# RWKV recurrence: the triangular inverse by substitution in 16x16 blocks and one Newton step

## The chip, the cores and the metric

One core of a Trainium2 chip runs the whole program. The metric is device time in microseconds, the median of the runs shown; lower is better. TensorE (PE), VectorE (DVE), ScalarE (ACT), GpSimd (POOL) and the DMA queues (issued mostly by SP) each work through their own list of instructions in order and meet through semaphores.

## What is computed

The reference is a stack of transformer blocks in float32. Its first part has an attention layer, an RWKV-7 layer and two MLPs; a second part follows with further mixers and feed-forward layers. The change touches the RWKV-7 recurrence alone, which runs over 256 context tokens and 512 tokens, in both directions, for 16 heads of 64:

```python
def wkv_scan(r, w, k, v, a, b, s0, reverse):
    def step(s, inp):
        r_t, w_t, k_t, v_t, a_t, b_t = inp
        sa = jnp.einsum('bhvk,bhk->bhv', s, a_t)
        s = s * w_t[:, :, None, :] + sa[..., None] * b_t[:, :, None, :] + v_t[..., None] * k_t[:, :, None, :]
        return s, jnp.einsum('bhvk,bhk->bhv', s, r_t)
```

## The kernel before

The recurrence is computed in chunks of 64 tokens: 12 chunks ("slots") per direction and head. Inside a chunk the dependence of each step on the ones before it is a strictly triangular 64x64 matrix A, and the chunk needs the inverse of (I - A). `rwkv_wkv` (L1789) makes 8 passes, one for each pair of heads. A pass has 2 directions x 2 heads x 12 slots = 48 such matrices; direction d lies in partitions 64d to 64d + 63.

For a pass, `wkv_scores` (L1950) makes the matrices A and masks them into `GA` (VectorE, L1973) and the output factors into `E` (L1975). `wkv_inverse` (L2043) inverts the two 32x32 diagonal blocks of each matrix. It copies them into `Z` (ScalarE, L2048), transposes them on VectorE so that each of the 128 partitions holds one row index of the 24 matrices side by side (L2051, L2052), and then substitutes forward: 30 steps of a multiplication into `pr` (L2061) and an addition into `T` (L2062). Two transposes bring the result back as `TC` and as its turned form `TS` (L2066, L2067), and four copies on ScalarE put it on the diagonal of `TTt` (L2073). `wkv_cross` (L2077) then makes the off-diagonal 32x32 block of the 64x64 inverse with two groups of products of 32x32 matmuls, on two of the array's strips at a time (L2086 and L2087, L2098 and L2099), and evicts them on ScalarE and VectorE. After it come `wkv_transfer` (L2105: `pswu`, `psft`, the evictions `FC` and `FT`), `wkv_scan` (L2142: 11 chained steps `pstep` with the eviction `S` on ScalarE, and the outputs `psy` to `Y`) and, in the next pass, `wkv_readout` (L2205, partly on GpSimd).

The inverse of pass p + 1 is made during pass p. The order is written by hand: a string of letters, `WKV_ORDER` (L1451), or `WKV_LAST` (L1454) for the last pass, says which generator takes its next step, and `in_order` (L1855) spreads the steps of the inverse evenly between the letters:

```python
            while done < 34 and done * n <= 34 * j:
                next(inverse, None)
                done += 1
            if c in steps:
                with self.tc.issue_after(last):
                    next(steps[c], None)
```

Here y is the cross product, b the transposes of `BK` (`psbk`, L2037), m the products `psmv` (L2026), w the transfer, s the scan, z the readout of the pass before, g the scores, a and v two more sets of transposes. The recording layer may still move an instruction ahead of others on its engine. `TC` and `TS` share their buffers with tiles of the readout (tags `zz` and `ro`, one buffer each), and PSUM results rotate over six banks (`psum`, L1910). In the pass before the last, g is the last part of `ada`, a vector-matrix product whose weights are loaded then.

## Time and profile before

| | |
|---|---|
| median of 3 runs | 3828.26 us (3827.4 to 3834.72) |
| the profiled execution | 3828.17 us, span 3826.0 us |
| PE busy | 3610.4 us, 94% of the span |
| DVE busy | 2059.8 us, 54% |
| ACT busy | 1583.4 us, 41% |
| POOL busy | 728.8 us, 19% |

The span runs from the first to the last instruction of the profiled execution; the device time has a little around it. A busy share is an average over stages that differ in what holds them up. The recurrence takes about 500 us of the span, from about 1390 us on. A matmul of float32 operands leaves two MATMUL records in the trace, and its end is modelled, so records of neighbouring matmuls overlap: how fast a group runs is read from the distance of starts.

### The profile page before, as it was taken

What the parts mean: (1) busy time and instruction counts of PE and PEld (TensorE: products, weight loads), DVE (VectorE), ACT (ScalarE), POOL (GpSimd) and SP (SyncE); (2) the same over time, 40 slices, a digit from 0 to 9 for tenths busy, and PEclk for the clock granted to TensorE, in tenths of its full rate; (3) what the DMA queues carried; (4) which work ended last, traced back from release to release, by engine and by line L of the source; (5) the groups of instructions that cost most, each with busy time, mean ns of one, the idle gap of its engine ahead of it and who ended that gap; (6) DMA issues with size and microseconds to landing.
All of it is one profiled execution on the core that took longest, in us unless ns stands there. A gap on an engine that the chain in (4) does not pass through costs nothing.

```text
span 3826.0 us, 62818 instructions
## 1 busy us (share of the span) xinstructions
PE 3610.4 (94%) x25700; PEld 2920.4 (76%) x25700; DVE 2059.8 (54%) x3993; ACT 1583.4 (41%) x2988; POOL 728.8 (19%) x602
## 2 busy tenths in 40 slices
PE   7999999999898978888899999998999899989998
PEld 5777877888775657777688889888888788778886
DVE  5556433333557778778354345567434734474346
ACT  5555332122334656765442234354222444442233
POOL 2000033434212010001134430003111200031112
PEclk9999999999999988888899999999999999999999
DMA  5232233122232772232433332113333211133332
GB/s 180 64 94 96 73 101 99 60 67 63 73 106 93 272 267 75 94 94 88 156 103 94 94 99 84 44 57 100 92 96 100 88 59 53 53 92 90 99 96 69
DMA packets 308272, 370.76 MB, mean 97 GB/s; under 512 B 31768, under 2 KB 228368, under 8 KB 305936
## 3 DMA queue, kind: packets, MB, share of 16 engines
q1 hardware_dynamic: 298752, 340.28, 28.2%
q0 software_dynamic: 8976, 26.40, 2.2%
q8 instruction: 202, 3.31, 0.4%
q14 instruction: 86, 0.70, 0.1%
q10 hardware_dynamic: 256, 0.07, 0.0%
HBM read 324.72 MB, written 41.98 MB: 96 GB/s over the span
## 4 chain that ended last, share of the span: by engine, by line
PE 53%; DVE 9%; ACT 3%; issue 2%; DMA 1%; POOL 0%; SPq 0%; DVEq 0%; ACTq 0%; POOLq 0%
PE psu L144 5%; PE psu L143 5%; PE psu L142 5%; PE psy L144 5%; PE psy L143 4%; PE psy L142 4%; PE psj L144 4%; PE psj L143 4%; PE psj L142 4%; DVE T L2062 2%; PE S L973 2%; DVE pr L2061 2%; DVE Tlo L298 1%; ACT Z L2048 1%; PE psk L142 1%
## 5 line engine op out<-in xcount | busy, mean ns | idle before, releaser
L136 ACT CAST whi<-wraw 128x1024 fp32r<-128x1024 f32 (+1 forms) x402 | 417.0, 1039 | 922.0 <-PE psy L144 527.6
L137 DVE TENSOR_TENSOR wlo<-wraw,whi 128x1024 fp32r<-128x1024 f32 (+1 forms) x402 | 506.4, 1262 | 535.2 <-ACT whi L136 534.8
L142 PE MATMUL psu<-Thi,whi 128*128 128x512 f32 (+1 forms) x1408 | 498.5, 354 | 8.7 <-ACT r L334 6.0
L144 PE MATMUL psu<-Thi,wlo 128*128 128x512 f32 (+1 forms) x1408 | 500.0, 355 | 0.3 <-DVE wlo L137 0.3
L143 PE MATMUL psu<-Tlo,whi 128*128 128x512 f32 (+1 forms) x1408 | 497.9, 354 | 0.0
L142 PE MATMUL psj<-whi,Thi 128*128 128x256 f32 (+1 forms) x1568 | 482.1, 309 | 8.3 <-ACT whi L136 6.1
L144 PE MATMUL psj<-whi,Tlo 128*128 128x256 f32 (+1 forms) x1568 | 475.1, 304 | 2.9 <-DVE Tlo L298 2.6
L143 PE MATMUL psj<-wlo,Thi 128*128 128x256 f32 (+1 forms) x1568 | 475.9, 304 | 1.7 <-DVE wlo L137 1.6
L142 PE MATMUL psy<-whi,uh 128*128 128x512 f32 x1152 | 452.5, 393 | 2.8 <-ACT whi L136 2.7
L144 PE MATMUL psy<-whi,ul 128*128 128x512 f32 x1152 | 454.6, 395 | 0.0
L143 PE MATMUL psy<-wlo,uh 128*128 128x512 f32 x1152 | 452.1, 392 | 0.5 <-DVE wlo L137 0.5
L335 POOL TENSOR_TENSOR q<-r 128x512 f32<-128x512 f32 (+1 forms) x176 | 235.3, 1337 | 876.7 <-ACT r L334 876.6
L142 PEld LDWEIGHTS psj<-whi,Thi 128*128 128x128 f32 x1568 | 300.1, 192 | 23.1 <-ACT whi L136 7.2
L144 PEld LDWEIGHTS psj<-whi,Tlo 128*128 128x128 f32 x1568 | 299.2, 191 | 17.0 <-DVE Tlo L298 4.3
L143 PEld LDWEIGHTS psj<-wlo,Thi 128*128 128x128 f32 x1568 | 299.9, 191 | 15.2 <-DVE wlo L137 3.6
L142 PEld LDWEIGHTS psu<-Thi,whi 128*128 128x128 f32 x1408 | 266.9, 190 | 52.0 <-ACT r L334 8.1
L143 PEld LDWEIGHTS psu<-Tlo,whi 128*128 128x128 f32 x1408 | 267.1, 190 | 40.7
L144 PEld LDWEIGHTS psu<-Thi,wlo 128*128 128x128 f32 x1408 | 266.7, 189 | 38.6 <-DVE wlo L137 0.7
L337 DVE TENSOR_TENSOR ul<-q,uh 128x512 fp32r<-128x512 f32 (+1 forms) x176 | 104.6, 595 | 312.2 <-ACT uh L336 311.9
L144 PEld LDWEIGHTS psy<-whi,ul 128*128 128x128 f32 x1152 | 216.6, 188 | 52.9 <-DVE ul L337 6.5
L142 PEld LDWEIGHTS psy<-whi,uh 128*128 128x128 f32 x1152 | 216.8, 188 | 51.8 <-ACT whi L136 3.9
L143 PEld LDWEIGHTS psy<-wlo,uh 128*128 128x128 f32 x1152 | 216.6, 188 | 47.8 <-DVE wlo L137 0.8
(549 smaller groups left out, 6209.4 us busy)
## 6 DMA issues: line engine op xcount, KB each, us to landing
wraw<-in_mlp_w_dram SPq DMA_DIRECT2D x128, 512.0 KB
wraw<-in_ffn_w_dram SPq DMA_DIRECT2D x128, 512.0 KB
wraw<-in_ada_w_dram SPq DMA_DIRECT2D x64, 512.0 KB
wraw<-in_ev_w_in_dram SPq DMA_DIRECT2D x28, 512.0 KB
scr_bk<-BK SPq DMA_DIRECT2D x16, 768.0 KB
wraw<-in_od_w_in_dram SPq DMA_DIRECT2D x24, 512.0 KB
BK<-scr_bk SPq DMA_DIRECT2D x14, 768.0 KB
wraw<-in_rwkv_w_rkv_dram SPq DMA_DIRECT2D x16, 512.0 KB
```

The source lines that it names most:

```text
L136: nc.scalar.copy(hi, raw)
L137: nc.vector.tensor_tensor(lo, raw, hi.bitcast(F32), SUB)
L142: mm(ps, lhsT=ah, rhs=bh, start=start, stop=False)
L143: mm(ps, lhsT=ah, rhs=bl, start=False, stop=False)
L144: mm(ps, lhsT=al, rhs=bh, start=False, stop=stop)
L298: nc.vector.tensor_tensor(lo[k][:, s], t[:, :w], hi[k][:, s].bitcast(F32), SUB)
L335: nc.gpsimd.tensor_tensor(q[:, :w], r[:, :w], r[:, :w], MUL)
L337: nc.vector.tensor_tensor(ul[:, o:o + w], q[:, :w], uh[:, o:o + w].bitcast(F32), SUB)
L973: nc.tensor.matmul(S[:, :W], lhsT=q, rhs=k, start=True, stop=True)
L2048: nc.scalar.copy(Z[q, :, 0:24], GA[d][q, :, :, 32 * bl:32 * bl + 32].rearrange("p h s t -> p t (h s)"))
L2061: nc.vector.tensor_tensor(pv, T[:, j + 1:, j:j + 1].to_broadcast([P, n, j]), T[:, j:j + 1, 0:j].to_broadcast([P, n, j]), MUL)
L2062: nc.vector.tensor_tensor(T[:, j + 1:, 0:j], T[:, j + 1:, 0:j], pv, ADD)
```

## The change

VectorE now substitutes only in the two 16x16 diagonal blocks of each 32x32 block, both at once: 14 steps, over a view `B` of `T` that has the two blocks as one dimension. So `TC` and `TS` hold a block diagonal matrix X. A new generator, `wkv_merge`, makes the inverse of the 32x32 blocks by one Newton step, X (2I - (I - A) X), which is exact here because only one off-diagonal block is missing. For each head it accumulates 2I, -X and A X in one bank (`psn1`), with wide matmuls against the constant `two` and one 32x32 matmul per slot and strip, copies that to SBUF, multiplies it by X (`psn2`) and evicts the result straight into `TTt`; for the two strips that the cross product reads, it also makes the turned form (`psn3`) and writes it back into `TS` and `TC`. The four strips of the array take a matmul each in turn. The merge is made at the start of the pass itself, as four steps with the letter x ahead of the y steps. The four copies of L2073 are gone.

```diff
@@ -1448,10 +1448,10 @@
 
 
 
-WKV_ORDER = ("z b y b y b m y b m y b z b w w l z m w z m w s w z s w z s w w s w z s z z z s g v s g a s g s g v s g a "
+WKV_ORDER = ("x z x b x b x b y m y b y m y b z b w w l z m w z m w s w z s w z s w w s w z s z z z s g v s g a s g s g v s g a "
              "s g g v s g g a s g k r g g")
 
-WKV_LAST = "y m y m y y z w w z m w m z s w w s z w s z s w w w s s z s z z s z s r s q s q s q s q s"
+WKV_LAST = "x z x m x m x y y y y w w z m w m z s w w s z w s z s w w w s s z s z z s z s r s q s q s q s q s"
 LAST_PARTS = ((0, 4), (4, 8))
 WKV_FIRST = "f f f f f f f f b b b b b b"
 WKV_START = "l A A A v v v k c c . . . g g a g g c a g g c a g g c g g c g g c c c c"
@@ -1791,6 +1791,11 @@
         with ExitStack() as s:
             cp = self.pool(s, "wc", 1)
             self.Z = cp.tile([P, 32, 32], F32, name="Z")
+            self.two = cp.tile([P, 2, 32], F32, name="two")
+            for i in range(4):
+                q = slice(32 * i, 32 * i + 32)
+                for j, f in enumerate((2.0, -1.0)):
+                    nc.vector.tensor_scalar(self.two[q, j, :], self.ident[q, q], f, None, MUL)
 
             self.IR = cp.tile([P, 8, 3, 64], F32, name="IR")
 
@@ -1838,7 +1843,7 @@
                     pb = self.pb.pop()
                     bank = lambda name: pb.tile([P, 512], F32, name=name, tag="b")
                     ada = self.ada(1, (2,), bank, lambda: self.lt([P, 4, 2, 64], "DC").rearrange("p c i t -> p (c i t)"), self.wkv_raws)
-                steps = dict(m=self.wkv_fill_m(u[p]), y=self.wkv_cross(u[p]), w=self.wkv_transfer(u[p]), s=self.wkv_scan(u[p]), z=self.wkv_readout(u[p - 1]) if p else iter(()),
+                steps = dict(x=self.wkv_merge(u[p]), m=self.wkv_fill_m(u[p]), y=self.wkv_cross(u[p]), w=self.wkv_transfer(u[p]), s=self.wkv_scan(u[p]), z=self.wkv_readout(u[p - 1]) if p else iter(()),
                              l=self.wkv_next(u), k=self.wkv_next_v(u), r=self.wkv_next_r(u, p), g=self.wkv_scores_of(u, p + 2), a=self.wkv_fill_of(u, p + 2))
                 if p + 1 < KT:
                     steps.update(self.wkv_fill(u[p + 1]))
@@ -1858,7 +1863,7 @@
         for j, c in enumerate(order):
             traced = self.nc.cur_bb.bb.instructions
             last = next((i for i in reversed(traced) if i.engine == mybir.EngineType.PE), None)
-            while done < 34 and done * n <= 34 * j:
+            while done < 18 and done * n <= 18 * j:
                 next(inverse, None)
                 done += 1
             if c in steps:
@@ -2041,37 +2046,77 @@
 
 
     def wkv_inverse(self, u):
-        nc, tl, Z, GA, TTt = self.nc, self.wt, self.Z, u["GA"], self.TTt
+        nc, tl, Z, GA = self.nc, self.wt, self.Z, u["GA"]
         for d in range(2):
             for bl in range(2):
                 q = slice(64 * d + 32 * bl, 64 * d + 32 * bl + 32)
                 nc.scalar.copy(Z[q, :, 0:24], GA[d][q, :, :, 32 * bl:32 * bl + 32].rearrange("p h s t -> p t (h s)"))
         yield
-        T = tl([P, 32, 32], "T")
-        nc.vector.transpose(T[0:64].rearrange("p a b -> p (a b)"), Z[0:64].rearrange("p a b -> p (a b)"))
+        raw = tl([P, 33 * 32], "T")
+        flat = raw[:, :32 * 32]
+        T = flat.rearrange("p (a b) -> p a b", b=32)
+
+        B = raw.rearrange("p (x r) -> p x r", x=2)[:, :, :512].rearrange("p x (a b) -> p x a b", b=32)
+        nc.vector.transpose(flat[0:64], Z[0:64].rearrange("p a b -> p (a b)"))
         nc.vector.transpose(T[64:128].rearrange("p a b -> p b a"), Z[64:128])
-        dg = T.rearrange("p a b -> p (a b)")[:, 0:1024:33]
-        nc.vector.tensor_scalar(dg, dg, 1.0, None, ADD)
         yield
 
-        for j in range(1, 31):
-            n = 31 - j
-            pr = tl([P, 256], "pr")
-            pv = pr[:, :n * j].rearrange("p (a b) -> p a b", b=j)
-            nc.vector.tensor_tensor(pv, T[:, j + 1:, j:j + 1].to_broadcast([P, n, j]), T[:, j:j + 1, 0:j].to_broadcast([P, n, j]), MUL)
-            nc.vector.tensor_tensor(T[:, j + 1:, 0:j], T[:, j + 1:, 0:j], pv, ADD)
+        for j in range(1, 15):
+            n = 15 - j
+            pr = tl([P, 2 * 56], "pr")
+            pv = pr[:, :2 * n * j].rearrange("p (x a b) -> p x a b", x=2, b=j)
+            nc.vector.tensor_tensor(pv, B[:, :, j + 1:, j:j + 1].to_broadcast([P, 2, n, j]), B[:, :, j:j + 1, 0:j].to_broadcast([P, 2, n, j]), MUL)
+            nc.vector.tensor_tensor(B[:, :, j + 1:, 0:j], B[:, :, j + 1:, 0:j], pv, ADD)
             yield
+        nc.vector.memset(flat[:, 0:1024:33], 1.0)
         u["TC"] = TC = self.rt([P, 32, 32], "TC", tag="zz")
         u["TS"] = TS = self.rt([P, 32, 32], "TS", tag="ro")
-        nc.vector.transpose(TC.rearrange("p a b -> p (a b)"), T.rearrange("p a b -> p (a b)"))
+        nc.vector.transpose(TC.rearrange("p a b -> p (a b)"), flat)
+        yield
         nc.vector.transpose(TS, T.rearrange("p a b -> p b a"))
         yield
-        for d in range(2):
-            for bl in range(2):
-                q = slice(64 * d + 32 * bl, 64 * d + 32 * bl + 32)
-                src = TC if d == 0 else TS
-                nc.scalar.copy(TTt[q, :, :, 64 * d + 32 * bl:64 * d + 32 * bl + 32], src[q, :, 0:24].rearrange("p t (h s) -> p h s t", h=2))
-        yield
+
+
+
+    def wkv_merge(self, u):
+        nc, psum, GA, TTt, TC, TS = self.nc, self.psum, u["GA"], self.TTt, u["TC"], u["TS"]
+        plain, turned = (TS, TC), (TC, TS)
+        strips = [(slice(32 * i, 32 * i + 32), i // 2, i % 2) for i in range(4)]
+        n = NSLOT * 32
+        ws = []
+        for h in range(2):
+            ps = psum("psn1")
+            ms = slice(h * NSLOT, h * NSLOT + NSLOT)
+            for q, d, bl in strips:
+                last = nc.tensor.matmul(ps[q, :n], lhsT=self.two[q, 0, :], rhs=self.ident[q, q].unsqueeze(1).to_broadcast([32, NSLOT, 32]), start=True, stop=True, skip_group_check=True).ins
+            with self.tc.issue_after(last):
+                for q, d, bl in strips:
+                    nc.tensor.matmul(ps[q, :n], lhsT=self.two[q, 1, :], rhs=plain[d][q, :, ms].rearrange("p t s -> p s t"), start=False, stop=True, skip_group_check=True)
+                for sl in range(NSLOT):
+                    for q, d, bl in strips:
+                        nc.tensor.matmul(ps[q, 32 * sl:32 * sl + 32], lhsT=GA[d][q, h, sl, 32 * bl:32 * bl + 32], rhs=plain[d][q, :, h * NSLOT + sl],
+                                         start=False, stop=True, skip_group_check=True)
+            w = self.rt([P, SX], "y1s", 2)[:, :n]
+            nc.scalar.copy(w, ps[:, :n])
+            ws.append(w)
+            yield
+        for h, w in enumerate(ws):
+            ps, pn = psum("psn2"), psum("psn3")
+            ms = slice(h * NSLOT, h * NSLOT + NSLOT)
+            for sl in range(NSLOT):
+                c = slice(32 * sl, 32 * sl + 32)
+                for q, d, bl in strips:
+                    nc.tensor.matmul(ps[q, c], lhsT=w[q, c], rhs=turned[d][q, :, h * NSLOT + sl], start=True, stop=True)
+            for sl in range(NSLOT):
+                c = slice(32 * sl, 32 * sl + 32)
+                for q, d, bl in (strips[0], strips[3]):
+                    nc.tensor.matmul(pn[q, c], lhsT=turned[d][q, :, h * NSLOT + sl], rhs=w[q, c], start=True, stop=True)
+            for q, d, bl in (strips[0], strips[3]):
+                nc.scalar.copy(plain[d][q, :, ms], pn[q, :n].rearrange("p (s t) -> p t s", t=32))
+            for q, d, bl in strips:
+                put = nc.vector.tensor_copy if bl else nc.scalar.copy
+                put(TTt[q, h, :, 64 * d + 32 * bl:64 * d + 32 * bl + 32], ps[q, :n].rearrange("p (s t) -> p s t", t=32))
+            yield
 
 
     def wkv_cross(self, u):
```

On PE, at the border of two passes, `psy<-S,FT` is the last output of the scan. Before:

```order
L2160 MATMUL psy<-UV,E_12202 64x64 x2
L2160 MATMUL psy<-UV,E_12203 64x64 x2
L2173 MATMUL psy<-S,FT 64x64 x16
L2037 MATMUL psbk<-ident,BK_13734 128x128 x4
L2086 MATMUL psy_14345<-TS,GA_13219 32x32
```

and now:

```order
L2205 MATMUL psy<-UV,E_12211 64x64 x2
L2205 MATMUL psy<-UV,E_12212 64x64 x2
L2218 MATMUL psy<-S,FT 64x64 x16
L2091 MATMUL psn_14737<-ident,two 32x384 x4
L2094 MATMUL psn_14737<-TS,two 32x384 x2
L2094 MATMUL psn_14737<-TC,two 32x384 x2
L2097 MATMUL psn_14737<-TS,GA_13426 32x32 x2
L2097 MATMUL psn_14737<-TC,GA_13427 32x32 x2
```

The pass begins with the merge's wide matmuls and its small ones, where the cross product stood; the three other steps of the merge and the transposes between them follow before the cross product.

On VectorE, where the transfer's results `FC` and `FT` are evicted, substitution steps of the next pass stood among them:

```order
L2061 TENSOR_TENSOR pr<-T 128x240
L2062 TENSOR_TENSOR T<-T,pr 128x16x15
L2136 TENSOR_TENSOR FT<-psft,IR 128x512 x2
L2241 SCALAR_TENSOR_TENSOR z<-psz,ncol,bv 128x512
L2061 TENSOR_TENSOR pr<-T 128x240
L2062 TENSOR_TENSOR T<-T,pr 128x15x16
L2061 TENSOR_TENSOR pr<-T 128x238
L2062 TENSOR_TENSOR T<-T,pr 128x14x17
L2061 TENSOR_TENSOR pr<-T 128x234
```

and now:

```order
L2069 TENSOR_TENSOR T<-T,pr 128x2x14
L2118 COPY TTt<-psn_14957 32x12x32 x2
L2135 COPY y1s<-psy_15046 32x384
L2135 COPY y1s<-psy_15084 32x384
L2270 TENSOR_REDUCE vr<-ysq 128x16
L2146 COPY TTt<-psy_15121 32x12x32
L2271 TENSOR_SCALAR vr<-vr 128x16
L2146 COPY TTt<-psy_15158 32x12x32
L2272 RECIPROCAL vr<-vr 128x16
L2076 STREAM_TRANSPOSE TS<-T 128x1024
L2275 TENSOR_TENSOR Y<-Y,vr 128x1024
L2179 TENSOR_TENSOR FC<-psft,IR 128x256 x2
```

`FT` (L2181) and z (L2286) follow at once. The substitution's last step now stands ahead of the merge's last copies into `TTt`, and none of it is left among the evictions of the transfer.

The merge's first copy into `TTt` on VectorE is the one place where the two meet; 20 instructions of the same substitution stand ahead of these rows:

```order
L2068 TENSOR_TENSOR pr<-T 128x88
L2118 COPY TTt<-psn_14871 32x12x32
L2069 TENSOR_TENSOR T<-T,pr 128x2x4x11
L2068 TENSOR_TENSOR pr<-T 128x72
L2069 TENSOR_TENSOR T<-T,pr 128x2x3x12
L2068 TENSOR_TENSOR pr<-T 128x52
```

So 21 of the 28 instructions come before that copy.

## Rows read from the trace of the kernel before

**Rows 1.** The page: busy time of the engines, and the chain by engine.

```profile
PE 3610.4 (94%) x25700; PEld 2920.4 (76%) x25700; DVE 2059.8 (54%) x3993; ACT 1583.4 (41%) x2988; POOL 728.8 (19%) x602
...
PE 53%; DVE 9%; ACT 3%; issue 2%; DMA 1%; POOL 0%; SPq 0%; DVEq 0%; ACTq 0%; POOLq 0%
```

**Rows 2.** Busy by stretch: from:to, length, PE, PEld, DVE, ACT, POOL, clock, DMA.

```profile
1429.10:1772.00 342.90, 298.26 (x5746) 259.99 (x5746) 271.09 (x618) 230.58 (x456) 27.07 (x24) 0.84 0.27 82
1539.30:1596.80 57.50, 48.43 (x969) 42.37 (x968) 46.40 (x104) 38.12 (x77) 4.52 (x3) 0.88 0.28 87
1772.00:1840.50 68.50, 58.02 (x893) 39.26 (x892) 40.62 (x89) 33.34 (x71) 4.58 (x3) 0.80 0.44 142
```

**Rows 3.** Waits of PE, 1539.3 to 1596.8 us: total, times, longest.

```profile
PE pstep L2173 <- ACT S L2188: 2.4, 2, 2.0
PE psy L2099 <- DVE y1s L2090: 1.9, 1, 1.9
PE psat L2012 <- DVE E L1975: 1.6, 1, 1.6
PE psy L2160 <- DVE GA L1973: 1.4, 1, 1.4
PE pstep L2173 <- DVE FT L2136: 1.1, 1, 1.1
```

**Rows 4.** The chain of the same stretch, by line.

```profile
by line: DVE T L2062 15.0%; DVE pr L2061 13.8%; issue 11.5%; ACT Z L2048 11.4%; PE psbk L2037 5.1%; DVE FT L2136 4.3%; DVE T L2052 3.4%; PE pswu L2115 3.0%; PE psy L2099 2.6%; PE psy L2098 2.4%; DVE z L2241 2.3%; PE pstep L2173 2.2%; DVE TC
```

**Rows 5.** Groups by line, 1370 to 1900 us: busy us, mean ns.

```profile
L2062 DVE TENSOR_TENSOR T<-T,pr 128x30 f32<-128x30 f32 (+14 forms) x240 | 94.8, 395 | 7.0
L2061 DVE TENSOR_TENSOR pr<-T 128x30 f32<-128x30 f32 (+14 forms) x240 | 81.0, 337 | 6.7
...
L2073 ACT COPY TTt<-TC 32x768 f32<-32x768 f32 x16 | 24.6, 1538 | 7.4 <-DVE TC L2066 7.0
...
L2101 DVE COPY TTt<-psy 32x384 f32<-32x384 f32 x16 | 8.6, 560 | 3.0 <-ACT TTt L2100 2.7
...
L2100 ACT COPY TTt<-psy 32x384 f32<-32x384 f32 x16 | 7.4, 462 | 6.6 <-PE psy L2099 6.6
```

**Rows 6.** The same groups with shapes kept apart, VectorE.

```profile
L2061 DVE TENSOR_TENSOR pr<-T 128x108 f32<-128x108 f32 x16 | 4.3, 271 | 0.5
...
L2061 DVE TENSOR_TENSOR pr<-T 128x30 f32<-128x30 f32 x16 | 3.1, 194 | 0.3
```

**Rows 7.** PE in order of time: start us, length us, engine, what.

```profile
1392.97 1.92 PE L225 MATMUL psada<-E,silu 128*32 128x512 f32 x16
...
1406.83 0.69 PE L1967 MATMUL psg<-DC,BK 64*64 64x64 f32 x32
...
1539.34 0.22 PE L2086 MATMUL psy<-TS,GA 32*32 32x32 f32 x1
...
1540.64 0.23 PE L2087 MATMUL psy<-TC,GA 32*32 32x32 f32 x1
1540.80 0.66 PE L2037 MATMUL psbk<-ident,BK 128*128 128x128 f32 x4
...
1559.04 1.10 PE L2026 MATMUL psmv<-UV,GA 64*64 64x64 f32 x32
```

**Rows 8.** Busy time by stretch, as rows 2; the granted clock stands after POOL.

```profile
1539.30:1543.80 4.50, 4.21 (x105) 3.58 (x104) 1.53 (x2) 4.44 (x4) 0.00 (x0) 1.00 0.36 151
1543.80:1557.40 13.60, 11.32 (x156) 10.49 (x156) 11.02 (x24) 8.18 (x18) 1.90 (x1) 0.50 0.42 141
```

**Rows 9.** PE at 0.50: a transpose block; one cross line, first to last.

```profile
1548.85 1.11 PE L2037 MATMUL psbk<-ident,BK 128*128 128x128 f32 x4
...
L2098 PE MATMUL psy<-TTt,y1s x24: 236/236/255, 1550.9 to 1552.2; 32*32 32x32 f32 x24
```

**Rows 10.** VectorE in order of time, at the end of the first substitution.

```profile
1425.44 0.69 DVE L228 TENSOR_TENSOR FC<-psada,FC 128x512 f32<-128x512 f32 x1 [4.86 <-PE psada L225]
```

**Rows 11.** VectorE in order of time, at the start of a pass.

```profile
1543.51 1.94 DVE L2052 STREAM_TRANSPOSE T<-Z 64x1024 f32<-64x1024 f32 x1 [1.87 <-ACT Z L2048]
```

## Prediction

> **What bounds the kernel now.** I read four views in this order: the page, the busy time by stretch, PE's waits in one pass, and the chain of the same pass. The page shows PE at 94% of the span and 53% of the chain [rows 1]. The change lies in that stage alone, from about 1390 to 1885 us. The stretches cut it at the first cross matmul of each pass: six like passes of 57.2 us on average, one of 68.5 us that also loads ada weights, and a last one [rows 2]. In the six, PE is busy for 298.3 of 342.9 us and VectorE for 271.1. So PE is idle 44.6 us, or **7.4 us a pass**: that is the most that a faster VectorE and ScalarE can give back there. The pass from 1539.3 us, which I use as the specimen, is idle for 9.1 us, and its five longest waits make 8.4 us, all on ScalarE or VectorE [rows 2, 3]. The chain of the same pass says something else: the two lines of the substitution, L2061 and L2062, are 28.8% of it, 16.6 us [rows 4]. Both are true: two engines run side by side, each nearly full, and the chain follows the one that was late last. A gain on VectorE ends where PE's own work is reached.
>
> **What goes from VectorE and ScalarE.** The substitution now costs 94.8 + 81.0 = 175.8 us for 8 passes, 22.0 us each [rows 5]. The change leaves 14 steps of two instructions, with 28 to 112 elements. The rows of 30 and 108 elements took 194 and 271 ns [rows 6]; 28 instructions priced on the line through them make 6.8 us, so 15.2 us a pass leave VectorE. The merge brings it four copies like L2101 at 560 ns, 2.2 us. ScalarE loses four copies of TTt at 1.54 us (6.2 us) and gets ten of 0.46 us like L2100 (4.6 us) [rows 5]. Neither is what PE waits for longest afterwards, unless a wait below moves there. The eight small multiplications that build the factors 2 and -1 run once; I cost them at nothing, beside the projection's matmuls, and at 1.6 us if that cover were gone (eight at the 194 ns of the smallest row).
>
> **What PE gets.** Per pass, from the diff: 16 wide matmuls (32x384), 96 small ones in the first product, 96 in the second, 48 in the third. A small fp32 matmul leaves two records in the trace, so these 240 are 480 records.
> - *Two strips at a time* (third product). The first cross product has the same size on two strips: 48 records from 1539.34 to 1540.64 us, 27.7 ns each [rows 7]. 96 of them: 2.7 us.
> - *Four strips at a time* (first and second product). The trace has no such stretch. Two tiles of 64x64 (psmv at full clock, 32 records in 1.10 us, the last 0.22) take 28.4 ns, as two strips of 32x32 do, and four tiles of 64x64 (psg, 32 in 0.69, the last 0.22) take 15.2 ns [rows 7]. So I bound four strips by 15.2 and 27.7 ns, and take 17, near the four tiles, since size made no difference with two: 384 records, 6.5 us (5.8 to 10.6).
> - *Wide.* Eight ada matmuls of 512 columns on four column strips took 1.92 us [rows 7], 0.24 each; at 384 columns 0.18, and 16 make 2.9 us. At half clock twice that, 5.8; I keep 2.9 as the value.
> - *Changes between 128x128 blocks and strips:* after the last cross matmul of a group the next block begins 0.16 us later instead of 0.03 [rows 7]; four more such places, 0.6 us.
>
> Sum **12.7 us a pass**, with ends of 10.7 and 19.7 us. The Trainium skill, TensorE: Matmul & The Clock Gate (section "Wait — 56ns, not 53.3ns?"), states a floor of about 25 ns from start to start however small a matmul is. By it the four-strip records would cost 384 x 25 = 9.6 us, an estimate, and the pass 3 us more; the 15.2 ns of the four tiles speaks against the floor.
>
> **The clock.** In the specimen PE ran at 1.00 for 4.5 us (two groups of cross matmuls and two blocks of transposes), then at 0.50, which is 1.2 GHz, for 13.6 us [rows 8]. The merge puts up to 13 us of the same kind of small matmuls ahead of that. I expect the clock to fall during it and the low stretch to grow by some 10 us. Two strips do not mind (the second cross product, 24 + 24 records from 1550.9 to 1552.2 us at half clock, is as quick as the first at full clock), but a block of four transposes takes 1.11 instead of 0.66 us [rows 7, 9]. Three such blocks and one of psmv, which I price alike: **+2 us a pass** (0 to 4).
>
> **What comes back.** The rows of the new order show that after the merge VectorE goes straight from the transpose TS to FC, FT and z, where it had substitution steps between them. So the waits for FT, E and GA shrink, and the 2.4 us behind ScalarE go with the TTt copies that held the queue; the wait for y1s at the start of a pass is covered by merge matmuls. What is late next is the readout's zz on GpSimd and the transpose TC, which still stands between two evictions. Of 7.4 us I give back **6** and leave 1.4.
>
> **Sum.** Per pass 12.7 + 2 - 6 = +8.7, for six passes +52. The ada pass is idle for 10.5 us [rows 2] and may give back 7 of it: 12.7 + 1 - 7 = +7. The last pass has no substitution beside it to shed, so I give it back 2: 12.7 + 1 - 2 = +12. The first substitution stands before all passes, but when it was done VectorE waited 4.86 us for the ada matmuls [rows 10], so its end is set by them: -1 for the smaller queue behind. Together **+70 us**. The profiled execution took 3828.17 us (span 3826.0), within 0.1 us of the median of 3828.26, so I predict 3898 us. The same sum from the kind ends: 10.7 + 0.5 - 6.9 in the six passes gives +26, and +37 in all; 19.7 + 1 - 5 gives +94, and +127 in all.
>
> **The rivals.**
> - *The strips do not run beside each other* and the low clock covers the merge: the upper ends, 3955 us. For it: no four-strip row exists. Against: four tiles do run together. 14%.
> - *The clock holds.* If the wide matmuls keep PE at 1.00 through merge and cross, the low stretch goes. Of its 11.3 busy us [rows 8] the two groups of the second cross product (2.6) would not shrink and the rest would halve: -4.3. A pass is then 12.7 - 4.3 - 6 = +2.4, in all 14 + 3 + 8 - 1 = +24: 3852 us. Against: the fall came after just such small matmuls. 12%.
> - *PE has room* (the other sign). If busy records overstate PE's work, the merge fits into it and the shorter substitution shortens the pass. Weight loads were busy for only 42.4 of 57.5 us [rows 2], a room of 15.1 us, over the 12.7 that come. Then six passes lose their 6 us of waits, the ada pass 3, the start 1: 3788 us. It decides if merge records can slip between those of other groups, that is, if PE's pieces leave gaps. The chain's 28.8% speak for it; against it, the listed waits account for nearly the whole idle time, so no gap is unseen. The Trainium skill, Trainium Kernel Development and Optimization (Best Practices), has this rule: judge the distance from the roofline by weight-load busy time, not by matmul busy time. 8%.
> - *VectorE's queue holds the merge.* In the new order 21 of the 28 substitution instructions of the next pass stand ahead of the merge's first copy to TTt. They cannot start before the transpose from Z ends (1545.45 us in the specimen, 6.1 us into the pass [rows 11]); 21 at 0.26 us end at 11.6 us, when PE is at about 10. The bank that this copy frees is wanted six banks later. At worst 2 us a pass, +12: 3910 us. 6%.
>
> **How the numbers follow.** My case has 60%; its range by the ends above is 3865 to 3935. The range reaches from 3844, below the clock that holds, to 3956. Left out are "PE has room" (8%), the low half of "the clock holds" (5%) and the top of the first rival (6%). A measurement here can tell 0.2%, 7.7 us. Faster: 8% and a rest of 1, so 0.09. Within 0.2%: 0.05, from the low side of the clock that holds. Slower: 0.86.
>
> **What would show it.** PE busy per pass should rise by 12 to 15 us and the pass by 8 or 9; the merge's four-strip records should start 15 to 20 ns apart; L2068 and L2069 should take about 55 us for all 8 passes; waits for FT, S and y1s should nearly vanish; the 0.50 stretch should begin inside the merge. The prediction is wrong if passes get shorter than 57 us, if the clock stays at 1.00 through the merge, or if PE's idle time stays at 7 us.

## The result, and the profile after

The changed kernel took 3897.99 us (median of 4 runs, 3895.69 to 3902.12), the kernel before beside it 3827.83: a ratio of **1.0177** (95% interval 1.0161 to 1.0193). The forecast was 3898. The profiled execution has a span of 3896.8 us, 70.8 more than before. First the page: busy time of the engines, and the chain that ended last, by engine [rows 1].

```profile
PE 3701.6 (95%) x29796; PEld 2991.6 (77%) x29796; DVE 1976.8 (51%) x3777; ACT 1573.2 (40%) x3036; POOL 726.0 (19%) x602
...
PE 57%; DVE 6%; ACT 2%; issue 2%; DMA 2%; POOL 0%; SPq 0%; POOLq 0%; ACTq 0%; DVEq 0%
```

VectorE lost 83 us, TensorE gained 91, and the chain moved from VectorE to PE. Then the busy time by stretch, cut at the first merge matmul of each pass: the six like passes, the pass with the ada weights, and the specimen pass, here the one from 1560.93 us [rows 2].

```profile
1433.95:1819.25 385.30, 363.25 (x8818) 308.81 (x8817) 199.54 (x434) 217.33 (x488) 26.47 (x24) 0.87 0.25 74
1819.25:1898.00 78.75, 68.34 (x1412) 48.08 (x1408) 30.90 (x68) 32.43 (x77) 4.85 (x4) 0.85 0.39 126
1560.93:1625.00 64.07, 60.63 (x1480) 51.60 (x1481) 35.37 (x77) 36.80 (x82) 4.49 (x3) 0.87 0.26 79
```

The 70.8 us split into 4.8 before the first pass, 42.4 in the six, 10.3 in the ada pass and 13.3 behind it. In the six, PE is busy for 65.0 us more, and its idle time fell from 44.6 to 22.1 us. Which waits went is seen in PE's waits over the six passes (total, times, longest), of before and of after:

```profile
PE pstep L2173 <- ACT S L2188: 17.4, 9, 3.5
PE psy L2099 <- DVE y1s L2090: 7.7, 6, 2.0
PE pstep L2173 <- DVE FT L2136: 7.7, 6, 1.8
PE psy L2160 <- DVE GA L1973: 5.1, 5, 1.5
PE psat L2012 <- DVE E L1975: 4.4, 6, 1.6
```

```profile
PE psy L2131 <- DVE TTt L2118: 8.4, 5, 3.4
PE psn L2091 <- DVE E L1980: 2.6, 5, 0.5
PE pstep L2218 <- ACT S L2233: 2.4, 6, 0.4
PE psn L2113 <- issue: 2.3, 2, 1.2
PE psn L2109 <- issue: 1.8, 4, 0.8
PE psy L2144 <- DVE y1s L2135: 1.3, 1, 1.3
PE psat L2017 <- DVE E L1980: 1.0, 1, 1.0
```

FT, GA and the long S waits are gone, and y1s is down from 7.7 to 1.3 us. E keeps 3.6 of its 4.4 us, most of them now at the head of the merge. In place of the others stands one for the merge's own copies to TTt, on VectorE. ScalarE and VectorE in order of time show how it arises:

```profile
1570.87 0.47 ACT L2118 COPY TTt<-psn 32x384 f32<-32x384 f32 x1 [1.93 <-PE psn L2109]
...
1576.49 0.47 ACT L2118 COPY TTt<-psn 32x384 f32<-32x384 f32 x1 [3.35 <-DVE TTt L2118]
...
1575.91 0.55 DVE L2118 COPY TTt<-psn 32x384 f32<-32x384 f32 x1
```

The four copies of a head are written in turn: ScalarE, VectorE, ScalarE, VectorE. Each waits for the one ahead. VectorE comes to its first only at 1575.91, behind 21 substitution instructions of the next pass, and for the last 3.35 us before that copy's end ScalarE stands still with all that is queued on it.

The merge itself, as stretches of the first product of the two heads: wide matmuls, small ones, then both for the other head.

```profile
1560.93:1562.85 1.92, 1.92 (x17) 0.62 (x20) 1.85 (x6) 0.37 (x1) 0.00 (x0) 1.00 0.58 230
1562.85:1564.20 1.35, 1.35 (x99) 1.35 (x95) 0.00 (x0) 1.32 (x2) 0.00 (x0) 1.00 0.10 36
1564.21:1567.49 3.28, 3.28 (x126) 1.97 (x116) 2.44 (x2) 2.48 (x3) 0.00 (x0) 1.00 0.00 0
```

96 small records on four strips take 1.35 us, 14.1 ns each. Eight wide matmuls take 1.92, 0.24 each. The groups of one line show that these are of two kinds: the matmuls from the identity (L2091) last 481 ns in the record, those whose moving operand is read from the inverse with a step of 32 elements (L2094) 808.

```profile
L2091 PE MATMUL psn<-ident,two x8: 477/481/505, 1560.9 to 1561.3; 32*32 32x384 f32 x8
```

```profile
L2094 PE MATMUL psn<-TS,two x4: 797/808/817, 1561.6 to 1562.2; 32*32 32x384 f32 x4
```

Of the wide matmuls, four of L2091 fill 0.65 us (1560.93 to 1561.58), four of L2094 1.27 (to 1562.85). The Trainium skill, SBUF — State Buffer (section "Door 1: The DMA port swizzle"), says that accesses which leave a 16-byte line cost extra; a step of 32 floats does, and the trace agrees by this factor of two. The L2094 matmuls also add to what stands in the bank, but so do the ada matmuls of 512 columns in one piece, at 0.24 us each [rows 7]; no run changes the step alone.

The clock in the specimen pass [rows 8]:

```profile
1560.90:1573.60 12.70, 11.91 (x429) 8.58 (x430) 9.99 (x24) 6.66 (x9) 1.95 (x1) 1.00 0.11 42
1573.60:1590.70 17.10, 15.46 (x340) 14.17 (x338) 11.45 (x28) 8.76 (x18) 0.00 (x0) 0.50 0.29 85
```

It is 1.00 through the first 12.7 of the merge's 15.2 us (it ends at 1576.1) and 0.50 for 17 us from then on.

### The profile page after: what moved, and what is told of

Read it like the earlier page. It is cut to its first block, busy times and chain, and to the rows that moved or that the text cites. A ratio compares the mean times of both kernels' runs of the same rounds, so it can differ in the third digit from the quotient of the medians.

```text
span 3896.8 us, 70879 instructions
## 1 busy us (share of the span) xinstructions
PE 3701.6 (95%) x29796; PEld 2991.6 (77%) x29796; DVE 1976.8 (51%) x3777; ACT 1573.2 (40%) x3036; POOL 726.0 (19%) x602
## 4 chain that ended last, share of the span: by engine, by line
PE 57%; DVE 6%; ACT 2%; issue 2%; DMA 2%; POOL 0%; SPq 0%; POOLq 0%; ACTq 0%; DVEq 0%
PE psu L144 5%; PE psu L143 4%; PE psu L142 4%; PE psy L144 4%; PE psy L143 4%; PE psy L142 4%; PE psj L142 4%; PE psj L144 4%; PE psj L143 4%; PE S L973 2%; PE pswu L2160 1%; DVE Tlo L298 1%; PE psk L142 1%; PE psk L143 1%; PE psk L144 1%
```

## The experiments

The theory: TensorE's own work sets the pass, and relief elsewhere returns only PE's waits. The table has every run, with the ratio to the kernel before on the same chip; the last three columns are worked out from the six-pass stretch of each profile.

| run | ratio (95% interval) | pass, us | PE idle, us a pass | clock |
|---|---|---|---|---|
| before | 1 | 57.2 | 7.4 | 0.84 |
| changed | 1.0177 (1.0161 to 1.0193) | 64.2 | 3.7 | 0.87 |
| half only | 0.9946 (0.9931 to 0.9961) | 54.3 | 5.0 | 0.84 |
| full + merge | 1.0164 (1.0149 to 1.0179) | 65.0 | 4.4 | 0.86 |
| no wide | 1.0105 (1.0087 to 1.0124) | 60.8 | 3.4 | 0.81 |
| two strips | 1.0188 (1.0172 to 1.0203) | 66.4 | 1.3 | 0.82 |
| before, pool | 0.9944 (0.9932 to 0.9957) | 53.8 | 6.0 | 0.89 |
| copies on ACT | 1.0119 (1.0103 to 1.0134) | 61.7 | 2.0 | 0.89 |
| clearing late | 1.0165 (1.0151 to 1.0179) | 64.6 | 3.5 | 0.85 |
| small merge | 1.0035 (1.0022 to 1.0048) | 57.9 | 3.1 | 0.83 |
| half + pool | 0.9893 (0.9877 to 0.9908) | 50.5 | 2.6 | 0.87 |
| pool + cross | 0.9935 (0.9922 to 0.9947) | 53.3 | 5.7 | 0.90 |
| pool + cross + Z | **0.9888** (0.9872 to 0.9904) | 50.6 | 5.1 | 0.95 |
| small merge, cleared | 1.0040 (1.0027 to 1.0052) | 57.9 | 3.2 | 0.83 |

### The substitution and the merge apart

**Half only** puts the new loop into the kernel before:

```diff
-        for j in range(1, 31):
-            n = 31 - j
+        for j in range(1, 15):
+            n = 15 - j
...
```

> The kernel before with the shorter substitution alone: 14 steps inside the 16x16 blocks, no merge, the four copies to TTt on ScalarE kept. It leaves out the off-diagonal 16x16 blocks of the inverse. Theory (TensorE's own work sets the pass): PE busy per pass stays at 50 us; only waits can go, 3 to 5 of the 7.4 us a pass, so 20 to 30 us in the six passes, up to 5 in the ada pass: about 3800 us (3790 to 3812). Rival (the substitution, 28.8% of the chain, sets the pace): 15 us a pass come back in seven passes, below 3760 us. Rival (ScalarE's queue, which keeps its copies, sets the waits): no change, above 3818 us.

**Full + merge** does the reverse in the changed kernel: the loop to 31 again, with the merge behind it.

> The changed kernel with the full substitution of the kernel before in front of the merge (the Newton step then works on an inverse that is already done). Theory (TensorE sets the pass): VectorE has room for the 15 us a pass, so of the 3.8 us of waits per pass that the change gave back most return and nothing more: 20 to 35 us over the changed kernel, about 3925 us (3915 to 3940). Rival (the substitution sets the pace on VectorE): 15 us a pass in seven passes, about 4000 us. Rival (VectorE's length does not matter at all, the waits went with ScalarE's copies): within 8 us of 3898.

The six-pass stretches, of half only, then of full + merge, and PE's waits in the first:

```profile
1438.54:1764.47 325.93, 295.90 (x5745) 257.79 (x5745) 181.82 (x411) 224.18 (x452) 26.41 (x24) 0.84 0.28 86
```

```profile
1431.65:1821.37 389.72, 363.62 (x8818) 308.72 (x8817) 286.81 (x637) 217.61 (x488) 26.51 (x24) 0.86 0.24 73
```

```profile
PE pstep L2176 <- ACT S L2191: 19.3, 12, 3.5
PE psy L2102 <- DVE y1s L2093: 6.8, 5, 1.4
...
PE psbk L2037 <- DVE E L1975: 0.5, 1, 0.5
```

Half only is 0.54% faster, about 21 us: the waits for FT, GA and E are gone (0.5 us left of 17.2), those for S stay. VectorE gave up 89 us in six passes and PE took 17 of them. Behind the merge the short substitution is worth nothing that can be measured: with the full one the time is the same (the intervals overlap), and the pass 0.7 us longer. I had expected 20 to 35 us there; the rival that VectorE's length does not matter holds. With the full substitution PE waits 1.4 us for FT behind the merge, against 7.7 in the kernel before: the merge's own time on PE seems to cover what VectorE lacks.

### What the merge's matmuls cost

**No wide** drops the matmuls with 2 and -1; the small ones begin the sum.

```diff
-            for q, d, bl in strips:
-                last = nc.tensor.matmul(ps[q, :n], lhsT=self.two[q, 0, :], rhs=self.ident[q, q].unsqueeze(1).to_broadcast([32, NSLOT, 32]), start=True, stop=True, skip_group_check=True).ins
...
-                    nc.tensor.matmul(ps[q, :n], lhsT=self.two[q, 1, :], rhs=plain[d][q, :, ms].rearrange("p t s -> p s t"), start=False, stop=True, skip_group_check=True)
...
-                                         start=False, stop=True, skip_group_check=True)
+                                     start=True, stop=True)
```

> The changed kernel without the 16 wide matmuls of each merge (the part 2I - X of the Newton step is left out, so the product is N X alone). Theory (every microsecond of PE work in the merge is a microsecond of the pass): four sets of four at about 0.65 us, 2.6 us a pass, 8 passes: 21 us less, 3877 us (3870 to 3883). Rival (other work already sets the merge's stretch: the copies to TTt that alternate between ScalarE and VectorE): less than a third of that, above 3890 us.

**Two strips** takes the strips in pairs in the first two products:

```diff
+        pairs = [(sl, strips[i]) for pair in ((0, 3), (1, 2)) for sl in range(NSLOT) for i in pair]
-                for sl in range(NSLOT):
-                    for q, d, bl in strips:
+                for sl, (q, d, bl) in pairs:
```

> The changed kernel with the first and second product of the merge written for two strips at a time (all slots of strips 0 and 3, then of 1 and 2) in place of four. Theory: 28 ns a record in place of 14, so 384 records cost 5.3 us a pass more, 8 passes 42 us: 3940 us (3930 to 3948). Rival (the array takes a small record every 14 ns whatever strips it names): no change, within 8 us of 3898. Rival (the pass waits for the copies to TTt, not for these matmuls): below 3915 us.

Without the wide matmuls a pass is 3.4 us shorter, more than the 2.6 expected, less than the 3.84 (16 at 0.24) that they fill. PE's busy time fell by 3.1 of these: the clock, 0.81 in place of 0.87, takes part back. The merge as one stretch, of the changed kernel and without the wide matmuls:

```profile
1560.93:1576.11 15.18, 13.90 (x520) 10.52 (x520) 12.20 (x32) 6.66 (x9) 1.95 (x1) 0.92 0.10 36
```

```profile
1551.81:1565.20 13.39, 11.04 (x487) 9.95 (x488) 10.72 (x26) 7.71 (x12) 1.95 (x1) 0.59 0.10 37
```

With them PE holds 2.4 GHz through most of the merge, without them it falls into 1.2 GHz.

Two strips at a time: the first product of one head (the records of one operand: shortest, median, longest in ns, first and last start), then the six passes.

```profile
L2097 PE MATMUL psn<-TS,GA x47: 219/228/231, 1566.0 to 1568.4; 32*32 32x32 f32 x47
```

```profile
1430.05:1828.29 398.24, 390.69 (x8818) 339.84 (x8817) 199.45 (x434) 217.40 (x488) 26.43 (x24) 0.82 0.23 71
```

The 96 records of a head take 2.4 us in place of 1.35, 25 ns each (28 expected), so the strips do run beside each other when four are named. PE's busy time rose by 4.6 us a pass, and the pass by 2.2 only: of 398.24 us PE is idle for 7.6, and the waits for TTt are gone. So half of this extra work was hidden under waits, those for the copies (1.4 us a pass) above all, and the whole time cannot be told from the changed kernel's (1.0188 and 1.0177, 3930 to 3948 us expected). The theory in its bare form, every microsecond of PE work a microsecond of the pass, falls here: it holds only once such waits are used up.

### The waits, one by one

**Before, pool** changes one word, in the four copies to TTt:

```diff
-                nc.scalar.copy(TTt[q, :, :, 64 * d + 32 * bl:64 * d + 32 * bl + 32], src[q, :, 0:24].rearrange("p t (h s) -> p h s t", h=2))
+                nc.gpsimd.tensor_copy(TTt[q, :, :, 64 * d + 32 * bl:64 * d + 32 * bl + 32], src[q, :, 0:24].rearrange("p t (h s) -> p h s t", h=2))
```

> The kernel before, with the four copies to TTt of each pass (32x768, 1.5 us each on ScalarE) moved to GpSimd; nothing else. Theory (the waits that the change gave back belong to ScalarE's copies, not to the substitution): in the six passes PE waits 17.4 us for S before; they fall to 5 or less: 10 to 16 us less than before, 0.9958 to 0.9974 of it. Rival (the S waits belong to the other evictions in ScalarE's queue): within 5 us of before. Rival (GpSimd's copies hold VectorE's two-input work up, as its readout steps do): slower than before by over 5 us.

It is 0.56% faster than before, more than the 0.26 to 0.42% expected. PE's waits for S fell from 17.4 to 2.4 us, those for FT from 7.7 to 3.3, while those for E and GA grew (to 8.9 and 7.2):

```profile
PE pstep L2173 <- DVE FT L2136: 3.3, 6, 0.6
...
PE pstep L2173 <- ACT S L2188: 2.4, 6, 0.4
```

The six passes:

```profile
1431.38:1754.15 322.77, 286.51 (x5744) 249.89 (x5745) 271.24 (x614) 188.72 (x427) 67.71 (x51) 0.89 0.28 89
```

Of the 20.1 us only 8.4 are idle time. PE's busy time fell by 11.8 for the same matmuls, with the clock at 0.89 in place of 0.84. A late part of one pass, before and here:

```profile
1689.00:1713.90 24.90, 21.05 (x336) 17.72 (x336) 18.17 (x46) 18.12 (x31) 1.30 (x1) 0.79 0.32 87
```

```profile
1672.00:1699.30 27.30, 22.66 (x474) 18.91 (x473) 23.32 (x54) 14.55 (x35) 8.77 (x6) 1.00 0.33 97
```

Two of PE's waits in that pass of the kernel before bear on this:

```profile
PE pstep L2173 <- ACT S L2188: 2.9, 1, 2.9
PE pstep L2173 <- DVE FT L2136: 1.8, 1, 1.8
```

The granted clock fell from 1.00 to 0.50 at 1690.6 us, 1.6 us after the wait for FT had ended, and again at 1707.6, at the end of the wait for S. Here the same waits last 0.6 and 0.4 us, and the clock stays at 1.00. A wait of PE can be paid twice.

**Copies on ACT** lets ScalarE do all the merge's copies to TTt:

```diff
-                put = nc.vector.tensor_copy if bl else nc.scalar.copy
-                put(TTt[q, h, :, 64 * d + 32 * bl:64 * d + 32 * bl + 32], ps[q, :n].rearrange("p (s t) -> p s t", t=32))
+                nc.scalar.copy(TTt[q, h, :, 64 * d + 32 * bl:64 * d + 32 * bl + 32], ps[q, :n].rearrange("p (s t) -> p s t", t=32))
```

> The changed kernel with all copies of the merge to TTt on ScalarE (in place of a row of ScalarE, VectorE, ScalarE, VectorE). Theory: in that row ScalarE's third copy waits for VectorE's second, which stands behind substitution steps; PE's waits for TTt (8.4 us in the six passes, 2.6 in the ada pass) vanish: 6 to 11 us less than the changed kernel, 1.015 to 1.016 of before. Rival (another wait of the same length takes their place): the time of the changed kernel, 1.0177.

The waits for TTt vanish, and the gain is double the forecast: about 22 us by the ratios (0.58%). In the six passes 9.8 us of idle time go, and 5.4 us of busy time with the clock (0.87 to 0.89). Of the rest 2.1 us lie in the ada pass, and 2.8 ahead of the first merge, where the two kernels are alike.

**Clearing late** moves one line behind the call that starts the recurrence:

```diff
-            nc.gpsimd.memset(self.TTt, 0.0)
...
             self.pb.append(pb)
+            nc.gpsimd.memset(self.TTt, 0.0)
```

> The changed kernel with GpSimd's clearing of TTt (2.68 us) put after the stage that starts the recurrence, away from VectorE's eight small multiplications. Theory (two of those multiplications waited for GpSimd's clearing to end: 3.1 us each, side by side, against 0.17 for the other six): the eight take 0.9 us in place of 3.94. The time moves by 0 to 3 us, which this measurement hardly tells. Rival (the long multiplications are code loading or DMA traffic, not GpSimd): they stay at about 3 us.

VectorE and GpSimd in order of time in the changed kernel, then VectorE's eight multiplications in this one (shortest, median, longest, ns):

```profile
1371.06 3.94 DVE L1798 TENSOR_SCALAR two<-ident 32x32 f32<-32x32 f32 x8
...
1371.71 2.68 POOL L1826 MEMSET TTt<- 128x3072 f32 x1
```

```profile
L1798 DVE TENSOR_SCALAR two<-ident x8: 162/168/178, 1365.8 to 1366.7; 32x32 f32<-32x32 f32 x8
```

The stall was GpSimd's. But the clearing, which now begins at 1372.66 us, holds VectorE's next copies in its place: the two into `IR` take 3.35 us from 1372.68, against 0.84 in the changed kernel. The time can't be told from the changed kernel's.

**Small merge** asks how little the merge can cost: no wide matmuls, no third product.

```diff
+                nc.vector.scalar_tensor_tensor(w[q, :, o], in0=ps[q, :n].rearrange("p (s t) -> p s t", t=32)[:, :, o], scalar=self.low[q, :],
+                                               in1=self.idl[q, o].unsqueeze(1).to_broadcast([64, NSLOT, 16]), op0=MUL, op1=ADD)
...
-                    nc.tensor.matmul(pn[q, c], lhsT=turned[d][q, :, h * NSLOT + sl], rhs=w[q, c], start=True, stop=True)
...
-                nc.scalar.copy(plain[d][q, :, ms], pn[q, :n].rearrange("p (s t) -> p t s", t=32))
+                nc.vector.transpose(plain[d][q, :, ms].rearrange("p t s -> p s t"), ps[q, :n].rearrange("p (s t) -> p s t", t=32))
```

> The changed kernel with a merge that needs only the off-diagonal block: the first product without the wide matmuls, VectorE forms I + that block, the second product as before, and the third product replaced by two transposes on VectorE; all copies to TTt on ScalarE. Same result. Theory (the pass follows PE's work): 2.6 us of wide matmuls and 2.7 us of two-strip records leave each pass, and the TTt waits: 5.5 to 6.5 us a pass, 8 passes, 44 to 52 us less than the changed kernel: 3846 to 3856 us, 1.005 to 1.007 of before, still slower than before. Rival (the chain merge, eviction, merge, eviction then sets the pace): over 3870 us. Rival (the shorter substitution pays once the merge is small): below 3828 us.

This kernel leaves the unfinished off-diagonal block in the inverse that enters the merge, so its merge computes another off-diagonal block than the text ahead says. **Small merge, cleared** sets the block to zero first:

```diff
         nc.vector.memset(flat[:, 0:1024:33], 1.0)
+        nc.vector.memset(T[:, 16:, 0:16], 0.0)
```

> The small merge (no wide matmuls, third product as transposes on VectorE, copies to TTt on ScalarE) with the off-diagonal block of the half-finished inverse set to zero before it, by one VectorE instruction of 256 elements a pass, so that I plus the masked product is the whole Newton factor. Theory: that instruction is hidden, so the time of the run without it, 1.0035 of before (1.002 to 1.005): the shorter substitution with the smallest merge that I found is still not faster than the full substitution. Rival: faster than before by over 0.2%.

Both end at the same place (1.005 to 1.007 had been expected for the first): 1.4% below the changed kernel, still 0.4% above the kernel before.

### Do the two reliefs add, and is there more

**Half + pool** joins the first and the fifth run.

> The kernel before with both reliefs and no merge: the shorter substitution (off-diagonal 16x16 blocks of the inverse left out) and the copies to TTt on GpSimd. Alone they gave -0.54% and -0.56%. Theory (they end different waits of PE: VectorE's FT, E and GA, and ScalarE's S with the clock that falls behind it): they add, 0.988 to 0.991 of before, about 3790 us; then the merge itself costs the changed kernel some 108 us, over 13 us a pass. Rival (both feed on the same idle time): 0.993 to 0.995, no better than either.

```profile
1437.14:1739.84 302.70, 287.30 (x5745) 250.89 (x5745) 181.75 (x410) 188.44 (x428) 63.06 (x48) 0.87 0.31 94
```

They add: -1.07%. Against this run the merge costs the changed kernel 1.0177 - 0.9893 = 2.84%, 109 us, of which 82.6 lie in the six passes, 13.8 a pass. This includes the new order of the letters, which no run has without a merge.

**Pool + cross** and **pool + cross + Z** leave the full substitution and the kernel before as they are, and move copies:

```diff
-            nc.vector.tensor_copy(y1s[q2, :], y1[q2, :384])
+            nc.scalar.copy(y1s[q2, :], y1[q2, :384])
...
-            nc.vector.tensor_copy(TTt[q3, h, :, 64:96], y2[q3, :384].rearrange("p (s t) -> p s t", t=32))
+            nc.scalar.copy(TTt[q3, h, :, 64:96], y2[q3, :384].rearrange("p (s t) -> p s t", t=32))
```

> The kernel before with the copies to TTt on GpSimd and VectorE's copies of the two cross products (y1s and TTt of strips 2 and 3) on ScalarE as well. Theory (two engines that share one tile's copies make PE wait for the one with the longer queue, here VectorE's substitution): the 10.7 us that PE waits for y1s in the six passes fall to under 5, 5 to 10 us less than with the copies on GpSimd alone: 0.992 to 0.993 of before. Rival (two copies in a row on ScalarE are later than two side by side): 0.995 or more.

```diff
-                nc.scalar.copy(Z[q, :, 0:24], GA[d][q, :, :, 32 * bl:32 * bl + 32].rearrange("p h s t -> p t (h s)"))
+                put = nc.gpsimd.tensor_copy if bl else nc.scalar.copy
+                put(Z[q, :, 0:24], GA[d][q, :, :, 32 * bl:32 * bl + 32].rearrange("p h s t -> p t (h s)"))
```

> As the run with both moves, and two of the four copies into Z (1.5 us each on ScalarE, ahead of each substitution) on GpSimd. Theory (the substitution starts some 3 us earlier, so VectorE reaches GA, E and FT earlier): the 22 us that PE waits for these in the six passes halve: 0.988 to 0.991 of before, about 3793 us. Rival (PE's work and the cover of the other waits already set the pass): within 0.15% of the run without it.

```profile
1433.49:1736.92 303.43, 273.04 (x5746) 236.20 (x5745) 257.52 (x589) 180.23 (x441) 79.45 (x57) 0.95 0.29 93
```

The cross copies gave nothing on top that can be told from pool alone (0.9935, 0.992 to 0.993 expected). With Z shared as well, the kernel is 1.12% faster than before and 2.8% faster than the changed one. The waits for GA, E and FT did not halve as expected (21.9 to 18.6 us in the six passes; PE idle 5.7 to 5.1 us a pass); PE's busy time fell instead, 285.1 to 273.0 us, at a clock of 0.95. What in the new timing holds the clock up was not tried further.

## Why the prediction was right

The direction and the mechanism in the main were right: added work on a nearly full PE, less the waits that go. Several terms of the sum were not right, and that the total was met to the microsecond is luck: the six passes grew by 9.6 us less than forecast, the rest by 10.4 more.

- **PE's work, 12.7 us a pass:** right in its total. By the rows above it is 384 records at 14.1 ns (5.4, forecast 6.5), 96 at 28 ns (2.7), 16 wide ones at 0.24 us (3.84, forecast 2.9) and the switches (0.6, kept): 12.5. The wide term was mis-sized: the row it came from has its moving operand in one piece, and the half of these matmuls that read it so took 0.16 us each, the other half 0.32. The low end of this sum, 10.7, does not come out of its terms, which give 12.0 with four strips at 15.2 ns. The floor of 25 ns from start to start that the Trainium skill states (TensorE: Matmul & The Clock Gate, section "Wait — 56ns, not 53.3ns?") does not hold for the records of four strips, as the prediction counted them; a whole float32 matmul of two records takes 28.2 ns there.
- **The clock, +2 us:** this step failed. I let the clock fall in the first steps of the merge; in the specimen pass it fell near its end. Over the six passes it rose from 0.84 to 0.87: about 110 of 342.9 us were at 1.2 GHz before and 102 of 385.3 after, where some 10 us more a pass had been forecast. PE's busy time rose by 10.8 us a pass, less than the 12 to 15 that were to show the forecast; 12.5 came, and the 1.7 that are missing are put down to the clock. The rival "the clock holds" had its mechanism right and its price too large: the low stretch moved back, it did not go.
- **What comes back, 6 of 7.4 us:** only 3.8 came. I named zz and the transpose TC as late next; it was the alternating copies, which VectorE reached 15.0 us into the pass and not at 11.6: its transpose from Z ended 1.2 us later than in the specimen of before, and GpSimd held one of the 21 instructions for 1.6 us (last section). That is the rival "VectorE's queue holds the merge", costed at 12 us at worst and in the trace at 11 us of PE's waits (8.4, and the 2.6 in the ada pass below); taking it away returned 22 us, in part for the clock's sake.
- **Per pass** 12.5 - 1.7 - 3.8 = 7.0 against 7.1 measured and 8.7 forecast. They close by construction, since 1.7 is what is left between 12.5 and PE's busy time.
- **The ada pass, 7 of 10.5 us back:** this step failed too; nothing came back. PE's idle time stayed at 10.4 us and the pass grew by 10.3 (forecast 7). Of the 10.5 before, 6.6 were waits for the DMA of the ada weights, which a shorter VectorE queue does not end. The first two lines are of before; the third, of after, is a new wait for the merge's copies:

```profile
PE psada L225 <- DMA DA<-in_ada_w_dram: 3.9, 2, 2.1
PE psada L225 <- DMA BK<-in_ada_w_dram: 2.7, 2, 1.6
```

```profile
PE psbk L2042 <- DVE TTt L2118: 2.6, 1, 2.6
```

- **Behind the ada pass** +13.3 (forecast 12).
- **The start, -1 us:** +4.8 in the one profile of each kernel. VectorE was 2.0 us late ahead of the multiplications (1370.45 against 1368.46 us for the same instruction), where the kernels are alike; behind them it was 5.8 us late (BK at 1375.03 against 1369.27): the stall that I had costed at nothing. That it reaches the first merge is not shown. From the first multiplication to the first merge matmul the changed kernel took 62.9 us, the run with the late clearing 61.5, and four other runs with the stall (full + merge, no wide, two strips, copies on ACT) 59.3 to 64.0; PE waits for ada weights in between.
- **Why there is relief at all.** I gave the returned waits to the shorter substitution and to ScalarE's lighter queue together. Apart they are 0.54% and 0.56%; behind the merge the first is worth nothing that can be measured.
- **"PE has room"** falls. Read from the busy time of weight loads, the room was 15.1 us a pass; 13.8 us is what the merge costs. The Trainium skill, Trainium Kernel Development and Optimization (Best Practices), names weight-load busy time together with MFU (the share of peak arithmetic reached) for the distance from the roofline; as a measure of room in a pass the trace does not bear it out.
- **L2068 and L2069**, forecast 55 us, took 36.5 + 27.3 = 63.8 [rows 5 has the lines of before]: six instructions of 1.78 us in place of 0.21, below, are 9.4 of it.

## What to carry to other kernels

An engine that is next to full takes added work almost one to one once its waits are used up, and what a faster neighbour returns is bounded by the waits for that neighbour alone: price each wait by its releaser before crediting a relief to it. Copies of one tile that alternate between engines run at the pace of the longest queue. Look for the engine that is idle: here GpSimd took four 1.5 us copies a pass from ScalarE, and that was worth as much as 15 us a pass taken from VectorE (0.56 and 0.54%).

## What the runs showed of the hardware

**GpSimd can stop VectorE.** VectorE and GpSimd in order of time, in the specimen pass of the changed kernel:

```profile
1568.81 1.78 DVE L2068 TENSOR_TENSOR pr<-T 128x52 f32<-128x52 f32 x1
...
1568.57 1.95 POOL L2266 TENSOR_TENSOR Y<-Y,mn 128x1024 f32<-128x1024 f32 x1 [23.45 <-DVE pr L2068]
```

The instruction of 52 elements needs 0.21 us a moment later; it ended at 1570.59, when GpSimd's subtraction had ended at 1570.52. The same happened in six passes of the eight. In the kernel before it happened two or three times in each of these:

```profile
1511.32 1.36 DVE L2061 TENSOR_TENSOR pr<-T 128x238 f32<-128x238 f32 x1
...
1511.05 1.36 POOL L2243 TENSOR_TENSOR zz<-zz,z 128x512 f32<-128x512 f32 x1 [18.64 <-DVE z L2241]
```

The Trainium skill, SBUF — State Buffer (section "Who interferes with whom"), states this: a VectorE instruction with two inputs in SBUF contends with a GpSimd instruction that reads SBUF, not with one that only writes it; copies and tensor_scalar can run in modes that need the whole pair of ports shared with GpSimd, and are then blocked while GpSimd has it. The trace agrees on each: the multiplications of the start are tensor_scalar, and GpSimd's clearing only writes. The start of the kernel before shows the other half: beside GpSimd's clearing the two-input BK ran on, and the copy behind it was held until the clearing ended (1372.40 us).

```profile
1370.14 0.95 DVE L1769 TENSOR_TENSOR BK<-sig,t 128x768 f32<-128x768 f32 x1
1371.01 1.43 DVE L1770 COPY phi<-E 128x12 f32<-128x12 f32 x1
...
1369.72 2.68 POOL L1821 MEMSET TTt<- 128x3072 f32 x1
```

**Four 32x32 strips take a record every 14.1 ns, two strips one every 25 to 28**, and the clock makes no difference: 96 records of the second product at 1.2 GHz, one head of the next pass in the changed kernel, as a stretch [rows 9 show two strips]:

```profile
1637.61:1638.97 1.36, 1.36 (x97) 1.36 (x98) 1.22 (x5) 0.03 (x1) 0.00 (x0) 0.50 0.00 0
```

PE's waits marked "issue" inside the merge (4.1 us in the six passes) are not explained by any run. They are 10.2 us without the wide matmuls, and none are listed with two strips at a time.
